# Thresholded attention on one core: a new table for the order of all instructions

## The chip, the core and the metric

The kernel runs on one core of one Trainium2 chip. Five engines work side by side: TensorE (PE, matmuls into PSUM), VectorE (DVE), ScalarE (ACT), GpSimd (POOL), and SyncE (SP), which here only issues transfers. The metric is the device time of one execution in microseconds.

## The reference

```python
batch, heads, seq, dim = 8, 12, 512, 64      # Q, K, V: float32, standard normal
scores = np.einsum('bhqd,bhkd->bhqk', Q, K) * scale            # scale = 1/8
weights = np.exp(scores - np.max(scores, axis=-1, keepdims=True))
weights = weights / (np.sum(weights, axis=-1, keepdims=True) + 1e-10)
weights = np.where(weights > threshold, weights, 0)            # threshold = 0.1
weights = weights / (np.sum(weights, axis=-1, keepdims=True) + 1e-10)
return np.einsum('bhqk,bhkd->bhqd', weights, V).astype(np.float32)
```

With 512 keys per query hardly any weight is over 0.1. A query row without such a weight has an output of zero.

## The kernel before

The kernel fills the output with zeros, finds the few query rows that can have a weight over the threshold, and computes those rows exactly. The 96 heads are 48 pairs, two pairs are a quad, and there are 24 quads. In what follows "quad q", "pair hp" and "key tile t" (0 to 3) number the work.

For each quad SP loads K (four transfers of 128 KB, `load_k`, line 330) and Q (`load_q`, line 334); for quads 0 and 1 the loads are split by pair, and some can stand on ACT's queue. PE transposes K in float32 (`do_ktr`, line 381), ACT or DVE evacuates it (`do_kev`, lines 389 and 391), POOL (for early quads also ACT or DVE) casts it to half precision (`do_kh`, lines 396, 398, 400). Q is cast first (`do_qcast`, lines 367, 369, 371), transposed in half precision (`do_qtr`, line 410) and evacuated by DVE (`do_qev`, line 416). Then come 192 score steps (`do_sc`, line 438: one key tile of one pair, two matmuls, one per head), 384 exponentials (`do_ex`: ACT at line 447 with the true exponential, DVE at line 449 with a bit trick that makes about the same number), and 192 row sum steps (`do_sm`, line 468: four matmuls that add the exponentials and their eighth powers, read from the same bits as bfloat16). A bound on the norms of Q and K needs squares of both ("bits", `do_bits`: POOL at line 425, ACT at 427, DVE at 429) and products with ones (`do_norms`, line 478).

The pairs form three groups of 24, 16 and 8. When a group's sums are complete, DVE (the first step, `do_y`, also on ACT: lines 486 and 488) compares the two sums (`do_d`, line 495; `do_fl`, line 500) and takes the eight best columns of each row (`do_mx`, line 504): the query rows that may survive. They are worked on in six stages of 8 pairs (three for group 0, two for group 1, one for group 2): an index product (`do_m`, line 513; `do_ix`, line 519), the index (`do_qi`, line 524), an indirect fetch of the query rows on POOL's queue (`do_gq`, line 534), their transposition with a mask (`do_xm`, line 541; `do_xev`, lines 547 and 549), the exact scores in float32 (`do_xqk`, line 556, 16 matmuls), the exponential with its sum (`do_xexp`, line 562), threshold and key number (lines 566 to 580), an indirect fetch of the value row (`do_gv`, line 585) and an indirect store to the output (`do_scatter`, line 600). The blank fills of the output ("z", `do_zero`, line 607, 512 KB each) stand on SP's queue.

Two helpers keep TensorE's clock up: eight warming steps of four matmuls on a blank tile (`do_warm`, line 340) at the start, and four spare products at the end (`do_spare`, line 344).

What sets the order: every one of the 1,326 steps is registered with its engines, its dependencies and the buffers that it takes and gives, and then issued one after the other as the string ORDER (line 13) says. Each word of it is a step's number in base 36 and a letter for the engine (P PE, V DVE, A ACT, G POOL, S SP, Q ACT's transfer queue, N none). So the table sets three things at once: the order on each engine's queue, which engine takes a step that several can do, and which buffer of a pool a step gets, since buffers are handed out first in, first out. Pools are short: seven PSUM banks ("one") for scores, transposes and stages, 32 buffers ("big") for K, Q and their forms. Transfers use eight semaphores in turn, so that the ninth waits for the landing of the first.

Of the kernel before, what the change touches and what calls it, by code (L numbers as in the profile page):

```python
# [9 lines left out]

ORDER = """6N fS gQ 1G hS 18Q 7P 24S 22S 8P 3G 5V 23S 16Q 9P 17S aP jP 2tS bP kA lV 2uS iG mA 2vS nP cP oV 3qS pV qP 3pS 12P sA rV yP dP 10A zV 26P 13A 25G 27V 1aP 28A 1bA 29V 0G 2aP uP 1cV 19A eP 2bV wA 52S 2cV 1eP 14V 2wG vA 2hP 1fV 1dG tP 2jA 11P 1gV 31P 2iA 1xG 2xP 32V 1tP 2yV 2zA 2lP 33V 30A 1pP 1vV xP 1qA 1uV 38P 2mA 3rG 3aV 1hP 1rA 53S 3sG 1wP 39V 1jA 3gP 1yG 6fS 15P 1iA 2nV 34P 3iA 3hV 2dP 36A 3cP 2fV 2eA 3tP 3kG 3dV 35A 6gS 2oP 3uA 3vV 1lP 2pP 7sS 1zN 1mA 1nV 3yP 3eA 3wG 3zV 56P 2qA 40V 3xG 57A 58V 45P 41P 46A 47V 1oP 54G 49P 42A 2rV 1kP 55G 4bA 2gP 43V 4lP 4aA 59G 95S 5bP 4nA 37P 3lG 5cV 1sP 4mA 4dP 5dV 4tP 4eA 4fV 6jP 4vA 4uV 5qP 6kA 3bP 5aG 3mN 5sV 2kP 6lA 5mP 6hG 5uP 5rA 5nV 5eP 6iG 7tS 5oA 4gP 5wV 4cP 5fA 6mG 5iP 96S 5gV 6oP 5vA 6nG aiS 4oP 6pV 5kA 4pP 6qV 7wP 5jA 7nV 6vP 7xA 7yV 5lP 7oG 5xP 4rA 44P 6xV 5yP 6wA d8S 5tP 60V 5zA 7fP 6zP 4qA 7hV 5hP 3jP 7gA 70V 7jP 99P 7kA 71V 77P 9aA 5pP 7uG 78V 7iP 79A 6yP 7vG 7lV 66P 9bA 7zG 81P 67A 7bP 82V 68A 3fP 97G 6rP 83V 7dA 98G ajS 2sP 7cV 6sA 88P 80G 8cP bwS 6tV 89A 7mP 9cG 9eP bvS 8eV 8aA 73P 9dG 8dA 7eP 7pN 9fV amP 4xG 75A 9gV 74V a5P anA 8kP a7V aoA 4wP 69P 8mA d9S 7aP 8lV 62P apG a6A 84P fzS 64V 8gP 86A 76P elS 85V 72P 8hA 48P 4hP 8iA 63V 9lP 4jA a8P akG 9mV 87P 9nA 9pP alG 4iV 8sP 9rA 8fP 6aG 8tV 8oP 9qA arP 8pA 65P asV a9P 8uA atV 8nP aaV 8qA auP 4yG 9hP awA abV b6P emS avA 4kP 9jV 61P 4sP 9iA fyS b7V b2P b8A dcP bxG 4zN b3V b4A acP byG ddA a1P deV bzP a2A aqG a3V 9xP 9oP daG c0V c1A ayP 9yA 8bP b0V 9zA a4P c2G biP 9tP azV 6bG bkA c4P 9sP c5V bjA axP 9vV 8vP hbS 9uA 8wP baP c6V 8xA 8jP 8yV dfG 6cN cfP bcA epP bbV dgG cgA cbP chV eqA dbG beP cdA 8rP ccV c3G 9kP bgA dhP bfV adG cjP erA 9wP hcS diV ckA cvP clV czP 21S cxA 8zP djV ciP d0A ioS ceP d1V esG ecP cwA bmP g0G edV dkP eeA bhP etG bdP boA bnV b9P dmA enG crP dlV doP ctA cmP k1S eoG csV e4P dqA cnP dpV e5A b1P 6uP efP coA e6V euP cpA dsP bqV e8P evV dtA cyP g1G e9V drP duA blP g2P ewV eaA brV exP g3A g4V fdP bsN aeG bpP ffA cuP ezV ipS f5P feA flP lfS f7V f6A cqP dnP k2S ebP eyV fmA g5G afN g7P fnA f1P g8V f9P hdG f2A dvP g9V e7P heG faA f3V c7P giP g6G fbA c9V foP a0P gjA 90G f0P gkV c8A fhP hfP fiV fjA isP hgV hhA b5P itA leS 91G iuV dwP gaP dxA gqP gcV fcP gbA f8P f4P grV dyA d2P h2P gsV iqG 92N geP h3A fpP ekS h4V ivG dzP ggA fgP gdP 51S irG frV gfA gtP gmP fqV hiG hkP goA guP k3G hlV ghP gwA fsP hmV glP hjG gnA e0P gvV gyP 2G e2A hnP gzV gpP e1A gxP h0V caP hpA ixP hzP hoA iyV lgG i7P i1A h1P izV h5P k4G e3P i8A i9V fkP lhG i0A qvS hvP xtV j4P iwG hwA 20P tlS 7qP xuV j5A 4G btP 3nP msS hxA k5P xvN xwV piS j6A j8P xxV 50P k6A mrS agP 93P k7A xyV jcP j9A xzP 6dP y0V jeA ydV i3P xrV y2G jdA hqP i2P y1V i5A jaV ibP 3oS ifP i4A jfP k8G igV o5S joP idA hyP ijG icV ihA yeP hrP jqA yfV iiP ygV htA hsV kaP liP jpA kbV jgP yhG ikV ljA iaP kcV ilN jkP lkA jhV khP jiA huP egG jmV y3P kiA kjA jlV jsP j0P h6A y4V klP j1V kkP y5P k9G ehA j2V ysV kmA jtV eiN juA jwV ktP knA o4S mtG yiP kuV y6A d3G kpP yjV h7A l1P kvV ykP y7V l2V krA h8N l3A y8V phS llG kqA lnP lmG ylA kxP loV mvP muG kzA ymV lpV ieP d4G kyA ynV ksP jnP mwA uxS m2P mxV meP m4A m6P m3V l4P mgA koP pjG n0P d5N mfV m7A lyP m8A myG jrP n1V o8P m0V lzA o6G s8S kdP n2V o9A o7G maP quS kfV j7P oaA mzG jvP mcV keA n7P jxG n3P mbA n8V m1P m5P n4A l0P n5V ytP n9A nbP plP s7S yuV ncV ndA lqP obG jyN pmA lsV nnP mmG pnA mdP n6P yvV lrV noA nvP l5P npA nxV odP 7rS l6A neP oeV m9P ocG l7A 6eS nwV luP miP pkG lwA d7S ofV nqP j3P mjV mkA qwG ogP mqS pqP lvA ohV poG nrP 94S oiA mhP qxG prV naP nsA tkS osP psV ywG ooP ntA otV jbP ltP opA kgP oqV ptP ouA mnG qyP yoV puV pvA q1P qzA l8P q2V orP q3A lxP r0V ldS p0P owP ppG p1A okP moN y9V p2V pwP oyA s9G mlP i6P omV uyS olA saG p8P qdP oxV paA sbP nzG qfA p9V nfP buS scA ozP ngV onP qeA ojP sdV qlP nhA q5P r1G k0S yxP qmV q6A r2G q7V r3P yyA p4P seG qnA r4V nuP haS p5A ftG q9P r5V pxP qbA qaV jjP p3P pzA q8P pyV riP p6A njP rkV sgP rjA yqG nyP shV nkA qgP ryP siV nlA r6P srP tmG rzA yzP ssV r8A ybG stV r7A s0V p7P yaV z0A ovP fuV waS reP ypV fvN tfV rqP rgA toP z1V rfV sfG rrA pbP z2V uzG r9P rsA qoP tnG rmP tpV tqA t3P s6S roA q4P t5V ttP trG t4A o3S nmP tuV tsG rnA qhP ahS ruP tvV qjA v0G niP rwV pgS u4P qiA ycG twP z3V u5V rvA kwP q0P rpP txA u6V t7P o0G tyA raP t9V uoP t8A rlP uqV qcP rbA v1P rcA upV u8P v2A usG rtP o1N z4V v3V sjP tjS u9A szP skV wbS uaA rdP rxP t0A t1V fxS snP u0P slA v4G s1P spV inS rhP u2A qkP utG u1V uwS v6P z7A svP v7V weP swA z8V wfA ugP v8V z9N smP wgA sxV v5G u3P suP soA z5G uhV ucP vtP uiA tzP ueV t6P udA w1P zaV vuA vxP sqP vzA ufP w2V wcG ujP vyA taP vvV whG v9P w9S qtS w3A vpP wiG vbV vaA vdP u7P wdG vrV vfA vwP ubP s2G vqA zbV wjP ukP veA vsP wkV uuN umA vlP ulV vhP vmA vgP wlV w0P vjA vnV s3G tbP wuP viA tdV unP voP wwA t2P wvV tcA wmP xmS x2P zcV woA x6P yrG s4N vcP x4A x8V w4P urP x3A wxP wnV wyP x7A wqP x0V zdP wzA x5P syP zeV wrA vkP pcV xeP wsA zgG xaP xgV teP xfA wpP x9P xcV xbA x1P xhP pdA zrV wtP z6G w5V xdP zsP 106A peN zhP ztV 107V d6P ziA ejP zvG zjP 108N 109V 10aV 10bV zuV 10cP zkA 10dV zwP zlV 10fG zmV jzP zxA s5P l9A zyP znV zfV zoV xiA zpG laA 10gP pfP 10hV zzA lbN 10iP qpA 100V 101V zqG 103V tgV 102V imP thN fwP 10jA xnP 104G o2P w6A uvP 10kV 10lV lcP tiP h9P qqA w7N w8P 10mV 10eV 10sV xjV 10oG 10nV xkN qrN 10rV xlP mpP qsP xoP xsV xpP xqP 105G 10qV 10tV 10pG"""


class Plan:
# [11 lines left out]
    def order(self):  # L28
        words = ORDER.split()
        if words:  # L30
            at = {"P": "PE", "V": "DVE", "A": "ACT", "G": "POOL", "S": "SP", "Q": "ACTQ", "N": "NONE"}
            seq = [(int(w[:-1], 36), at[w[-1]]) for w in words]
        else:
            seq = self.simple()
        assert sorted(i for i, _ in seq) == list(range(len(self.ops))), "the table is of other steps"
        idle = {p: list(range(k)) for p, k in self.pools.items()}
        self.held, done = {}, set()
        for i, e in seq:
            name, engs, _, deps, _, fn, takes, gives, _ = self.ops[i]
            assert e in engs and all(self.ids[d] in done for d in deps), name  # L40
            for pool, key in takes:
                self.held[pool, key] = idle[pool].pop(0)
            fn(e)
            for pool, key in gives:
                idle[pool].append(self.held[pool, key])
            done.add(i)
# [807 lines left out]
```

## Time and profile before

| | us |
|---|---|
| median of 3 runs | 172.88 (172.75 to 175.5) |
| the profiled execution | 172.14 |
| its span, first to last instruction | 170.4 |
| PE busy | 159.7 (94%) |
| ACT busy | 151.5 (89%) |
| DVE busy | 150.3 (88%) |
| POOL busy | 132.2 (78%) |
| DMA: moved | 38.27 MB, mean 225 GB/s |

Times in the rows are in microseconds from the span's start, except "mean ns". A busy PE is not a PE at its peak, since matmuls overlap in the records. Instructions of ACT and DVE overlap a little too, so that a row that merges many ("x18") shows what one costs when they follow each other closely. In square brackets stand the idle time of the engine before the row and what ended it.

### The profile page before, as it was taken

The numbers are of one execution on the slowest core, as the hardware profiler recorded it, in microseconds if no ns is written. First come the engines' busy times: TensorE is split into PE (matmuls) and PEld (weight loads), VectorE is DVE, ScalarE is ACT, GpSimd is POOL, SyncE is SP. The second block draws the span as 40 slices with busy tenths as digits, with TensorE's granted clock in tenths as the row PEclk, the third lists the DMA queues.
The fourth block names the chain that finished last, engine by engine and source line by source line (L and its number), as shares of the span: only waits on it lengthen the run. The fifth ranks groups of instructions, "written<-read, shape, count | busy, mean of one in ns | idle before, by whom it ended". The sixth has DMA issues, their size and how long they took to land.

```text
span 170.4 us, 5820 instructions
## 1 busy us (share of the span) xinstructions
PE 159.7 (94%) x2190; PEld 62.4 (37%) x2190; DVE 150.3 (88%) x349; ACT 151.5 (89%) x298; POOL 132.2 (78%) x200
## 2 busy tenths in 40 slices
PE   4999999999999999999979999999999999989970
PEld 1342544442444244333332344433343423332330
DVE  5489999989999999998989899999899999976570
ACT  3499999999999999899999999999899999956830
POOL 8549995795989759967693999999789969554362
PEclk9999999999999999999999999999999999999998
DMA  5999998969999797996995789999999997000000
GB/s 133 271 287 183 260 252 227 243 145 313 256 260 215 187 255 165 311 322 220 313 281 170 162 212 232 310 390 258 371 306 388 328 417 309 5 3 5 6 4 9
DMA packets 67453, 38.27 MB, mean 225 GB/s; under 512 B 51941, under 2 KB 64349, under 8 KB 67424
## 3 DMA queue, kind: packets, MB, share of 16 engines
q1 hardware_dynamic: 65520, 37.23, 78.4%
q10 hardware_dynamic: 1328, 0.52, 1.2%
q8 instruction: 17, 0.28, 0.7%
q0 software_dynamic: 576, 0.13, 0.5%
q14 instruction: 12, 0.10, 0.2%
HBM read 25.56 MB, written 12.78 MB: 225 GB/s over the span
## 4 chain that ended last, share of the span: by engine, by line
PE 69%; SPq 13%; DMA 7%; issue 3%; DVE 3%; ACT 2%; POOL 1%; ACTq 0%; POOLq 0%; DVEq 0%
PE sum L468 25%; PE one L438 25%; SPq L330 11%; PE one L556 5%; PE one L381 5%; DMA big<-in_K_dram 4%; PE one L410 3%; DMA big<-in_Q_dram 3%; SPq L334 2%; PE one L541 2%; PE one L478 2%; PE one L519 1%; POOL out_dram L600 1%; ACT e L447 1%; DVE junk L570 0%
## 5 line engine op out<-in xcount | busy, mean ns | idle before, releaser
L447 ACT ACTIVATE e<-one 128x512 f16<-128x512 f32 x232 | 119.6, 648 | 2.3 <-PE one L438 2.0
L449 DVE TENSOR_SCALAR e<-one 128x512 uint16<-128x512 f32 x152 | 97.0, 683 | 3.1 <-PE one L438 2.0
L438 PE MATMUL one<-big 64*128 64x512 f16 x384 | 67.2, 384 | 0.9 <-issue 0.3
L468 PE MATMUL sum<-e,w_s 128*32 128x512 f16 (+1 forms) x768 | 58.2, 384 | 0.0
L425 POOL TENSOR_TENSOR big<-big 128x512 bf16<-128x512 f16 x54 | 54.8, 1041 | 2.9 <-DVE big L429 2.8
L371 POOL CAST qh<-big 128x512 f16<-128x512 f32 x47 | 28.1, 616 | 14.4 <-PE one L438 5.1
L438 PEld LDWEIGHTS <-big 64*128 64x128 f16 x384 | 17.4, 95 | 34.3 <-issue 28.1
L400 POOL CAST big<-big 128x512 f16<-128x512 f32 x45 | 27.1, 615 | 2.7 <-DVE cut L566 1.3
L468 PEld LDWEIGHTS <-w_s 128*32 128x32 f16 (+1 forms) x768 | 15.5, 95 | 33.1 <-issue 27.9
L416 DVE COPY big<-one 128x512 f16<-128x512 f16 (+1 forms) x52 | 19.4, 398 | 2.1 <-PE one L410 1.6
L389 ACT COPY big<-one 128x512 f32<-128x512 f32 (+1 forms) x35 | 19.7, 600 | 1.3 <-PE one L381 1.2
L381 PE MATMUL one<-identity_f,big 64*128 64x64 f32 x384 | 18.3, 229 | 1.0 <-DMA big<-in_K_dram 0.7
L381 PEld LDWEIGHTS one<-identity_f,big 64*128 64x128 f32 x384 | 15.8, 140 | 6.7 <-POOL mask_x L225 1.6
L534 POOL DMA_INDIRECT qs<-in_Q_dram,idx x6 | 6.4, 1065 | 8.2 <-DVE idx L524 2.8
L391 DVE COPY big<-one 128x512 f32<-128x512 f32 (+1 forms) x17 | 10.5, 624 | 2.4 <-PE one L381 1.7
L556 PE MATMUL one<-big,xq 128*32 128x512 f32 x96 | 11.5, 597 | 0.6 <-issue 0.4
L410 PEld LDWEIGHTS <-qh 64*128 64x128 f16 x384 | 8.5, 95 | 8.2 <-issue 5.4
L410 PE MATMUL one<-identity_h,qh 64*128 64x64 f16 x384 | 10.7, 192 | 0.3 <-DVE big L391 0.2
L427 ACT ACTIVATE big<-big 128x1024 bf16<-128x1024 f16 x10 | 10.2, 1059 | 0.0
L600 POOL DMA_INDIRECT out_dram<-vr,idx x6 | 6.2, 1034 | 3.8 <-DVE cut L566 2.1
L585 POOL DMA_INDIRECT vr<-in_V_dram,idx x6 | 6.3, 1056 | 2.3 <-DVE oks L758 0.9
L562 ACT ACTIVATE one<-one 128x512 f32<-128x512 f32 x6 | 3.5, 582 | 4.2 <-PE one L556 4.2
(85 smaller groups left out, 81.3 us busy)
## 6 DMA issues: line engine op xcount, KB each, us to landing
out_dram<-zero SPq DMA_DIRECT2D x24, 512.0 KB
big<-in_K_dram SPq DMA_DIRECT2D x94, 128.0 KB
big<-in_Q_dram SPq DMA_DIRECT2D x22, 512.0 KB
big<-in_Q_dram SPq DMA_DIRECT2D x3, 256.0 KB
big<-in_K_dram ACTq DMA_DIRECT2D x2, 128.0 KB
big<-in_Q_dram ACTq DMA_DIRECT2D x1, 256.0 KB
qs<-in_Q_dram,idx POOLq DMA_INDIRECT x6, 3.8
vr<-in_V_dram,idx POOLq DMA_INDIRECT x6, 3.8
```

Source lines behind the costliest of these rows:

```text
L371: behind(nc.gpsimd.tensor_copy(dst, src))
L381: nc.tensor.matmul(dst[i][:, c:c + D], lhsT=src[ps, n0 + n, r, :], rhs=identity_f32[ps, ps], is_transpose=True, start=True, stop=True)
L389: nc.scalar.copy(dst, src)
L400: behind(nc.gpsimd.tensor_copy(dst, src))
L410: nc.tensor.matmul(dst[i][:, c:c + D], lhsT=src[ps, n0 + n, r, :], rhs=identity_h[ps, ps], is_transpose=True, start=True, stop=True)
L416: nc.vector.tensor_copy(qk_b[big("qk", q)][:, 0, n0:n0 + k, i * SO * D:(i + 1) * SO * D], src)
L425: behind(nc.gpsimd.tensor_tensor(out=dst[:, n, :], in0=src[:, n, :], in1=src[:, n, :], op=ALU.mult))
L438: nc.tensor.matmul(one[at("one", ("sc", hp, t, h))][:], lhsT=qk[ps, 1, n, t * P:(t + 1) * P], rhs=qk[ps, 0, n, :], start=True, stop=True)
L447: nc.scalar.activation(dst, src, ACTF.Exp, scale=scale, bias=-11.0 * math.log(2.0))
L449: nc.vector.tensor_scalar(dst.bitcast(u16), src, scale * LOG2E * 1024.0, 4096.0, op0=ALU.mult, op1=ALU.add)
L468: nc.tensor.matmul(dst[32 * j:32 * j + 32, :], lhsT=w, rhs=x, start=first, stop=False, skip_group_check=True)
L556: nc.tensor.matmul(one[at("one", ("xs", x))][sl, :], lhsT=xq_b[at("xq", x)][:, n, sl], rhs=kt_b[big("kt", quads[j])][:, n, :], start=(n == ...
```

## The change

The only line that changes is the table itself; the functions, the tiles and the steps stay as they are.

```diff
--- before.py
+++ after.py
@@ -10,7 +10,7 @@
-ORDER = """6N fS gQ 1G hS 18Q 7P 24S 22S 8P 3G 5V 23S 16Q 9P 17S aP jP 2tS bP kA lV 2uS iG mA 2vS ...
+ORDER = """6N fQ hS 1G gQ 24S 7P 18Q 22S 8P 9P 0G 5V 23S aP 16S 17Q bP cP 2vS dP iA 2tS jP nP kA lV ...
```

Counted from both tables, these steps are on another engine or in another stretch. "Start" is ahead of the first exponential in the table, "middle" from it to the last one, "tail" behind it.

| steps | before | now |
|---|---|---|
| exponentials ACT / DVE | 232 / 152 | 231 / 153 |
| squares ("bits") ACT / DVE / POOL | 10 / 11 / 27 | 8 / 14 / 26 |
| of these in the tail, ACT / DVE | 7 / 3 | 6 / 5 |
| evacuations of half a K tile in the middle, ACT / DVE | 3 / 3 | 5 / 1 |
| casts of K or Q by ACT: start / middle | 1 / 2 | 3 / 0 |
| casts of K or Q by DVE in the middle | 1 (K) | 1 (Q) |
| casts of K or Q by POOL | 92 | 92 |
| y of group 2 | ACT | DVE |
| transposed queries evacuated (xev) ACT / DVE | 3 / 3 | 4 / 2 |
| transfers on ACT's queue | 3 | 4 |
| warming steps ahead of the first transposes | 4 of 8 | 7 of 8 |
| score steps ahead of the second tile's transposes | 3 | 4 |
| exponentials left on ACT / DVE when stage 2's exact scores are issued | 2 / 3 | 3 / 2 |
| exponentials between the three fills ahead of the last K load and that load | 16 to 23 | 3 to 7 |

The first place is ACT's queue at the start of the program. `big` are loaded tiles, `qh` the cast Q, `one` PSUM banks, `e` the exponentials. Before:

```order
L330 DMA big_114<-in_K_dram 128x4x64
L334 DMA big_115<-in_Q_dram 128x2x256
L330 DMA big_114<-in_K_dram 128x4x64
L389 ACT_TABLE_LOAD
L389 COPY big_118<-one_107 128x256
L396 CAST big_119<-big_118 128x512
L447 ACTIVATE e_148<-one_112 128x512
```

Of the change, the same place:

```order
L330 DMA big_114<-in_K_dram 128x4x64 x2
L334 DMA big_115<-in_Q_dram 128x2x256
L330 DMA big_114<-in_K_dram 128x4x64
L367 ACT_TABLE_LOAD
L367 CAST qh_146<-big_115 128x512
L389 COPY big_118<-one_107 128x256
L396 CAST big_119<-big_118 128x512
L367 CAST qh_147<-big_116 128x512
L447 ACTIVATE e_149<-one_107 128x512
```

Both halves of K's first tile now come over ACT's queue, one after the other (the first Q tile has SP's first place instead), and two casts of Q stand ahead of the first exponential.

The second place is DVE's queue behind its last exponential: `y` holds the row sums of the last group, `idx_178` stage 4's index, `idx_179` stage 5's. Before:

```order
L449 TENSOR_SCALAR e_153<-one_110 128x512
L513 TENSOR_TENSOR m_166<-vals_164,mask_m 64x128
L429 TENSOR_SCALAR big_119<-big_141 128x512
L524 TENSOR_SCALAR idx_178<-one_106,base 128x1
L495 SCALAR_TENSOR_TENSOR y_162<-y_162,sum_113 64x512
L500 SCALAR_TENSOR_TENSOR y_162,count<-y_162,far_row 64x512
```

Of the change, the same place:

```order
L449 TENSOR_SCALAR e_156<-one_112 128x512
L429 TENSOR_SCALAR big_135<-big_116 128x512
L488 TENSOR_SCALAR y_162<-sum_113 64x512
L524 TENSOR_SCALAR idx_178<-one_110,base 128x1
L495 SCALAR_TENSOR_TENSOR y_162<-y_162,sum_113 64x512
L500 SCALAR_TENSOR_TENSOR y_162,count<-y_162,far_row 64x512
```

The step y (line 488) has come over from ACT and stands ahead of stage 4's index; the small product `m_166` was issued earlier.

The third place is POOL's queue in the same stretch: fetches of queries (`qs`), of values (`vr`) and the store of stage 2 (`vr_196`). One piece of the difference, before with -, now with +:

```order
 L534 DMA qs_183<-in_Q_dram,idx_177 128x64
+L534 DMA qs_184<-in_Q_dram,idx_178 128x64
 L600 DMA out_dram<-vr_196,idx_176 49152x64
-L534 DMA qs_184<-in_Q_dram,idx_178 128x64
 L534 DMA qs_185<-in_Q_dram,idx_179 128x64
 L585 DMA vr_197<-in_V_dram,idx_177 128x64
```

Stage 2's store stands behind stage 4's query fetch now, where it stood ahead of it.

## Rows read from the trace of the kernel before

**Rows 1.** Windows A:B: length, then PE, PEld, DVE, ACT, POOL busy, PEclk, DMA share, GB/s
```profile
7.20:10.00 2.80, 2.63 (x34) 1.02 (x30) 2.18 (x5) 2.53 (x6) 0.94 (x2) 1.00 1.28 241
7.20:149.70 142.50, 140.29 (x2006) 55.27 (x2004) 135.57 (x265) 139.28 (x280) 118.27 (x176) 1.00 0.92 258
149.70:170.40 20.70, 14.70 (x150) 5.25 (x141) 11.29 (x39) 9.95 (x16) 9.08 (x9) 0.97 0.03 6
```
**Rows 2.** Groups by line and form: busy us, mean ns of one, idle before
```profile
L391 DVE COPY big<-one 128x256 f32<-128x256 f32 x4 | 1.7, 423 | 1.8 <-PE one L381 1.7
L389 ACT COPY big<-one 128x256 f32<-128x256 f32 x4 | 1.5, 374 | 0.8 <-PE one L381 0.8
L396 ACT CAST big<-big 128x512 f16<-128x512 f32 x2 | 1.2, 620 | 0.4 <-DVE big L391 0.4
L367 ACT CAST qh<-big 128x512 f16<-128x512 f32 x1 | 0.6, 621 | 0.0
L429 DVE TENSOR_SCALAR big<-big 128x512 int32<-128x512 int32 x11 | 5.2, 472 | 0.1
```
**Rows 3.** Timeline (start us, us, instruction): the same instruction several times in a row
```profile
69.51 3.67 DVE L449 TENSOR_SCALAR e<-one 128x512 uint16<-128x512 f32 x6
140.56 9.06 ACT L447 ACTIVATE e<-one 128x512 f16<-128x512 f32 x18
155.60 2.95 ACT L427 ACTIVATE big<-big 128x1024 bf16<-128x1024 f16 x3
```
**Rows 4.** Timeline of the start, all engines
```profile
1.61 1.90 PE L340 MATMUL one<-blank,w_n 128*32 128x512 bf16 x16 [1.61 <-DVE w_n L210]
...
2.29 0.55 ACTq L330 DMA_DIRECT2D big<-in_K_dram  x1
...
2.87 1.28 ACT L389 ACT_TABLE_LOAD   x1 [2.87 <-issue]
...
4.21 0.69 PE L381 MATMUL one<-identity_f,big 64*128 64x64 f32 x8 [0.71 <-DMA big<-in_K_dram]
...
6.56 1.46 PE L438 MATMUL one<-big 64*128 64x512 f16 x6
...
7.18 0.69 DVE L449 TENSOR_SCALAR e<-one 128x512 uint16<-128x512 f32 x1 [0.67 <-PE one L438]
...
7.96 0.62 PE L340 MATMUL one<-blank,w_n 128*32 128x512 bf16 x4
...
10.13 0.40 PE L340 MATMUL one<-blank,w_n 128*32 128x512 bf16 x4
```
**Rows 5.** Timeline at stage 2's exact scores, PE and ACT
```profile
121.10 1.92 PE L556 MATMUL one<-big,xq 128*32 128x512 f32 x16
123.12 0.58 ACT L562 ACTIVATE one<-one 128x512 f32<-128x512 f32 x1 [0.66 <-PE one L556]
```
**Rows 6.** Timeline of the tail: POOL, ACT, DVE and PE
```profile
149.53 1.06 POOL L600 DMA_INDIRECT out_dram<-vr,idx  x1 [0.31 <-issue]
...
151.08 0.68 ACT L486 ACTIVATE y<-sum,small 64x512 f32<-64x512 f32 x1 [0.53 <-PE one L519]
151.20 0.22 DVE L524 TENSOR_SCALAR idx<-one,base 128x1 int32<-128x1 f32 x1 [0.73 <-PE one L519]
...
151.69 1.02 POOL L534 DMA_INDIRECT qs<-in_Q_dram,idx  x1 [1.10 <-DVE idx L524]
...
154.64 0.65 PE L541 MATMUL one<-mask_x,qs 128*64 128x256 f32 x4
...
155.24 1.00 POOL L534 DMA_INDIRECT qs<-in_Q_dram,idx  x1 [2.53 <-DVE cut L566]
```
**Rows 7.** SP's queue; a landing in the chain of waits; K's transposes by line
```profile
117.13 3.79 SPq L607 DMA_DIRECT2D out_dram<-zero  x3
122.18 3.18 SPq L330 DMA_DIRECT2D big<-in_K_dram  x4
...
29.57 7.55 DMA big<-in_K_dram
...
L381 PE MATMUL one<-identity_f,big x384: 216/222/367, 4.2 to 135.0; 64*128 64x64 f32 x192
```

2 lines of the change are left out of this document (1 added, 1 removed).

## The prediction

> **What bounds the kernel now.** I read the windows of the trace first, in three stretches: up to the first exponential at 7.2 us, to the end of the last one at 149.7, and the rest. In the middle 142.5 us ScalarE (ACT) is busy for 139.28 us and VectorE (DVE) for 135.57 [rows 1]. PE shows 140.29, but its matmuls overlap in the records, so that this says little of its load. The exponentials (line 447 on ACT, 449 on DVE) can run on either engine, so the two are one pool of work, and the middle lasts about half of their joint work plus their waits. Recorded idle time there is 3.2 us on ACT and 6.9 on DVE, 5.1 us on average: the most that a better order could win in the middle while it moves no work out. The DMA engines are 92% busy in the same stretch [rows 1], so transfers have little slack as a whole; but the view of waits names none for which ACT or DVE waited there.
>
> Then the timeline of the tail, 149.7 to 170.4. Nothing there is a matter of throughput: both engines are busy for about half of it [rows 1]. It is one chain: the last row sums, y, d, the search for survivors, the index product, the query fetch, the exact scores of stages 4 and 5, the value fetch, the store. So the order can change three things: how soon the first exponential starts, how much work and waiting lies in the middle, and how long the chain behind the last one is.
>
> **The change, part by part.** The sum is made against the profiled execution, 172.14 us, of which 170.4 are the span. That execution is 0.74 us faster than the median of the runs shown, 172.88.
>
> *The head.* Three rows set when the first transposes may start. Before, they begin at 4.21 us, on the arrival of K; the 16 warming products took 1.90 us from 1.61 [rows 4]. Now 28 of them stand ahead of the transposes: 28 × 1.90/16 = 3.33 us, so until 4.94. Also the second half of K's first tile has become the second transfer on ACT's queue, where it was the first before; this delays it towards the same time. And ACT issues four transfers instead of three, 0.55 us more [rows 4], ahead of the table load of 1.28 us, which now ends at 2.87 + 0.55 + 1.28 = 4.70; the cast of Q behind it takes 0.62 [rows 2] and ends at 5.32, before the transposes do. So transposes and first exponential come 4.94 − 4.21 = 0.73 us later, at about 7.9. Against this: in the 2.8 us from 7.2 to 10.0 ACT idles for 0.27 us and DVE for 0.62 [rows 1], since only three score products stand ahead of the next transposes; now there are four, which feed each engine with four exponentials. I count the average of that idle time, 0.45, as won. Head: +0.73 − 0.45 = **+0.28 us** (bounds: 0.73 if nothing is won back, −0.45 if the later start is made up by work that was done meanwhile).
>
> *Work in the middle.* By the table of step counts, between the first and the last exponential ACT loses one exponential ((9.06 − 0.65)/17 = 0.49 back to back [rows 3]), one squaring pass (0.95, half of 2.95 − 1.06 [rows 3]) and two casts (0.62 each [rows 2]; two casts of Q now stand ahead of the first exponential, in time in which ACT only waited), and takes over two evacuations of half a tile (0.37 each [rows 2]): −0.49 − 0.95 − 1.24 + 0.74 = −1.94 us. DVE gains one exponential ((3.67 − 0.68)/5 = 0.60 [rows 3]) and one bit pass (0.47 [rows 2]), loses two evacuations (0.42 each [rows 2]), and swaps one cast for another: +0.23 us. Together −1.71, half of it on each engine: **−0.86 us**. It is covered by nothing else: the work goes to time before the first exponential, and to the tail, where both engines have room. GpSimd (POOL) does one squaring less and as many casts; it is busy for 118.27 of 142.5 us, so its share doesn't decide.
>
> *Waits in the middle.* The clearest one is at stage 2's exact scores: PE spends 1.92 us on 16 fp32 products (line 556) and ACT waits 0.66 us for them [rows 5]. In the old order ACT has two exponentials left when that product is issued, in the new one three. One more is 0.49 us of the 0.66; DVE has one fewer, so I count half, **−0.24 us**. The other waits I can't read from the order; each is some tenths of a microsecond. Bounds for them: the average idle time of 5.1 us can shrink or grow by half, ±2.5; I take 0, since the order's other features (score products issued ahead, evacuations split in two) stay alike.
>
> *The tail.* Stage 2's store moves behind stage 4's query fetch on POOL's queue. Before, the store starts at 149.53 and takes 1.06 us, so it is over at 150.59; the fetch starts at 151.69, and what it waits for is DVE's index, written from 151.20 on [rows 6]. So the store wasn't in the way, and taking it away wins **nothing**. Behind the fetch it lies between 152.8 and 153.9, in the gap that POOL has until the next fetch at 155.24 [rows 6], and nothing of the chain waits for it. If that gap were gone, it would cost its 1.06 us.
>
> What does touch the chain is y, the first step on the sums of the last group. It moves from ACT to DVE, and DVE computes stage 4's index right behind it and ahead of d. Before, y ran on ACT from 151.08 and the index on DVE from 151.20, side by side [rows 6]. Now the index waits for y's 0.68 us: it starts at about 151.76, 0.56 later, and d is pushed by the distance from y's end, about 0.14 (the index takes 0.22 and overlaps its neighbours). The fetch is 0.56 later too; stage 4's mask product started at 154.64 [rows 6], held by the index product of stage 5 ahead of it on PE, which is only 0.14 later. Bounds: +0.14 if the fetch still has room, +0.56 if it has none; I take **+0.25 us**, nearer the first since PE was held by the other one. The squares left for the tail (11 where there were 10) run beside the chain on both engines.
>
> Sum: +0.28 − 0.86 − 0.24 + 0 + 0.25 = −0.57, 172.14 − 0.57 = **171.6 us**.
>
> **A rule weighed.** In the head, four warming products take 0.62 us at 7.96 and 0.40 at 10.13 [rows 4]: by its durations the first is TensorE at 1.2 GHz and the second at 2.4, though the column of the granted clock shows 1.00 in that stretch [rows 1]. PE had been busy with gaps before: until 3.51, then from 4.21. The Trainium skill ("TensorE: Matmul & The Clock Gate", Part 1) says that the low clock is the default and that sustained activity releases it. This trace agrees that it starts low. The new order puts the warming products in one unbroken run of 3.33 us; by the rule the clock may rise before the first score products, by the row it rises where it did. That is the second rival.
>
> **The rivals.**
> 1. *The order takes out more waits than can be read from it.* For it: 5.1 us of idle time on average, in many small pieces, which is what an order can remove. Against: the work is the same, and the longest pieces have other causes. Half of it gone: 171.6 − 2.5 = 169.1 us.
> 2. *The clock rises early.* The eight transposes take 0.69 us from 4.21; at the higher clock a group of four warming products goes from 0.62 to 0.40, by a third [rows 4]. A third of 0.69 and of the 0.62 us from the score's issue at 6.56 to the exponential at 7.18 is 0.44: 171.2 us.
> 3. *A transfer comes late* (the other side). Three blank fills of the output stand ahead of the last K load on SP's queue in both tables, but the new one issues them 13 to 16 exponentials later, close to that load. Three such took 3.79 us of SP's queue; before, the load followed them from 122.18 to 125.36 and was transposed by 135.0 [rows 7]. If all of their time is added, the issue ends at 129.15, 5.85 us ahead of the end of its use. This decides if a landing takes over about 5.5 us; a K load in the busy phase took 7.55 [rows 7]. Then the last scores are 2.0 us late: 173.6. Against: before, the issue ended 9.6 us ahead of the last transposes, and SP's queue need not be late by all of the 3.79.
> 4. *The clock falls or rises late.* No warming products are left between the first scores and the next transposes. Three more microseconds at 1.2 GHz would cost at most half of them: 173.1. Against: PE is dense there.
> 5. *The change does nothing*: the moved store is hidden before and after, and the rest cancels: 172.1.
>
> **How the numbers follow.** Forecast 0.45; rival 1 0.20; rival 2 0.12; rival 3 0.10; rival 4 0.05; rival 5 0.08. Differences under 2% can't be told from none on this kernel, whose own runs lie 1.6% apart. 2% below the median of before is 169.4, which about two thirds of rival 1 (0.13) and a little of the forecast and of rival 2 (0.03) pass: faster 0.16. 2% above is 176.3, for which rival 3 would have to hit several loads, 0.06 with what is left of rival 4; same 0.78. The forecast's own terms span 170.4 to 172.8. The range takes in rival 1 at its centre and rival 3 to one microsecond beyond: 168.8 to 174.5.
>
> **What would show it right or wrong.** The first exponential at 7.5 to 7.9 us (a time near 7.2 speaks for rival 2). From there to the last one 141 to 142 us, with ACT busy for about 2 us less in that stretch and no wait over 0.3 us before stage 2's exponential of exact scores. From the last exponential to the end 20.7 to 21.3 us, with d starting about 0.1 us after where y leaves it and POOL's store of stage 2 in a gap. Wrong: a wait of PE for a transfer of K beyond 20 us (rival 3), or idle time of ACT and DVE in the middle that differs by more than 2 us from 3.2 and 6.9 (rival 1, or its opposite).

## The result and the profile after the change

The changed kernel takes 172.25 us (median of 20 runs, 170.92 to 173.16), the kernel before 173.56 us (20 runs, 172.75 to 175.5, the three shown ahead of the prediction among them). The ratio is 0.992, with a 95% interval of 0.990 to 0.994: 0.8% or 1.3 us faster, no difference by the bound of 2%. The forecast was 171.6 us and no change. On a second chip the experiments give the same kernel 1.007 times the time of the one before (1.003 to 1.010). So the sum came out, several of its terms did not, and on the second chip the sign of the result is the other one.

The profiled execution after takes 172.26 us, with a span of 170.5. The windows of its trace, from the first exponential to the last and from there to the end, with busy time and instructions of each engine, granted clock, DMA share and GB/s, answer to [rows 1]:

```profile
core 0: us, PE busy (x) PEld busy (x) DVE busy (x) ACT busy (x) POOL busy (x), PEclk, DMA share, GB/s
8.98:150.15 141.17, 139.82 (x1998) 55.38 (x1996) 136.01 (x267) 137.54 (x278) 116.80 (x177) 1.00 0.90 256
150.15:170.50 20.35, 14.34 (x150) 5.26 (x142) 11.45 (x41) 8.36 (x15) 9.27 (x9) 0.92 0.03 6
```

The first exponential starts at 8.98 us where it was at 7.18 [rows 4]. The middle is 141.17 us long where it was 142.5 [rows 1]; ACT does 1.74 us less in it and DVE 0.44 more. Their idle time there is 3.63 and 5.16 us, where it was 3.2 and 6.9. So the middle, ACT's work and the idle time lie where the prediction put them; the first exponential (forecast 7.5 to 7.9) comes too late, and the tail, 20.35 us where it was 20.7, is shorter than the 20.7 to 21.3 of the forecast.

The start in the timeline of after (start, length, engine and line, operation; in brackets idle time and what ended it), with one row of the chain of work between:

```profile
0.75 1.33 ACTq L330 DMA_DIRECT2D big<-in_K_dram  x2
1.60 3.18 PE L340 MATMUL one<-blank,w_n 128*32 128x512 bf16 x28 [1.60 <-DVE w_n L210]
1.43 4.85 DMA big<-in_K_dram
6.42 0.69 PE L381 MATMUL one<-identity_f,big 64*128 64x64 f32 x8 [1.64 <-DMA big<-in_K_dram]
8.98 1.29 DVE L449 TENSOR_SCALAR e<-one 128x512 uint16<-128x512 f32 x2 [1.01 <-PE one L438]
```

The 28 warming products end at 4.78 us, as forecast (4.94). But the transposes then wait 1.64 us for the second half of K's first tile, the second transfer of ACT's queue, which lands at 6.28 (the first lands at 4.13). In the kernel before both halves were the first transfers of two queues, and the transposes began at 4.21 [rows 4].

The tail in the timeline of after answers to [rows 6]:

```profile
150.75 0.68 DVE L488 TENSOR_SCALAR y<-sum 64x512 f32<-64x512 f32 x1 [0.27 <-PE sum L468]
151.47 0.22 DVE L524 TENSOR_SCALAR idx<-one,base 128x1 int32<-128x1 f32 x1
151.72 0.69 DVE L495 SCALAR_TENSOR_TENSOR y<-y,sum 64x512 f32<-64x512 int32 x1
151.96 1.00 POOL L534 DMA_INDIRECT qs<-in_Q_dram,idx  x1 [2.31 <-DVE idx L524]
153.26 1.01 POOL L600 DMA_INDIRECT out_dram<-vr,idx  x1 [0.30 <-issue]
154.55 0.65 PE L541 MATMUL one<-mask_x,qs 128*64 128x256 f32 x4
```

The index stands between y and d (0.97 us from one to the other), and the store lies in POOL's gap, both as forecast. Not forecast: y starts 0.60 us after the last exponential's end; in the trace of before this was 1.39 us.

### The profile page after: what moved, and what is told of

The parts are those of the page before. It is cut to its first block, busy times and chain, and to the rows that moved or that the text cites. A ratio compares the mean times of both kernels' runs of the same rounds, so it can differ in the third digit from the quotient of the medians.

```text
span 170.5 us, 5813 instructions
## 1 busy us (share of the span) xinstructions
PE 159.4 (94%) x2190; PEld 62.8 (37%) x2190; DVE 150.8 (88%) x351; ACT 149.3 (88%) x297; POOL 130.1 (76%) x198
## 4 chain that ended last, share of the span: by engine, by line
PE 74%; DVE 12%; DMA 7%; ACT 3%; issue 1%; POOL 1%; ACTq 0%; DVEq 0%
PE sum L468 27%; PE one L438 26%; PE one L381 8%; DVE e L449 5%; DMA qs<-in_Q_dram,idx 4%; PE one L410 4%; PE one L556 3%; PE one L478 3%; DMA big<-in_K_dram 3%; ACT e L447 2%; PE one L541 1%; DVE nmax L491 1%; PE one L344 1%; DVE m L513 1%; DVE idx L524 1%
## 5 line engine op out<-in xcount | busy, mean ns | idle before, releaser
L468 PE MATMUL sum<-e,w_s 128*32 128x512 f16 (+1 forms) x768 | 59.4, 387 | 0.6 <-ACT e L447 0.4
L425 POOL TENSOR_TENSOR big<-big 128x512 bf16<-128x512 f16 x52 | 52.8, 1036 | 1.8 <-DVE big L429 1.3
L400 POOL CAST big<-big 128x512 f16<-128x512 f32 x47 | 28.1, 611 | 16.0 <-ACT big L389 4.4
L371 POOL CAST qh<-big 128x512 f16<-128x512 f32 x45 | 26.6, 611 | 6.3 <-DMA big<-in_Q_dram 3.3
L389 ACT COPY big<-one 128x512 f32<-128x512 f32 (+1 forms) x37 | 20.6, 598 | 2.9 <-PE one L381 2.7
L416 DVE COPY big<-one 128x512 f16<-128x512 f16 (+1 forms) x52 | 19.4, 398 | 1.7 <-issue 0.4
L391 DVE COPY big<-one 128x512 f32<-128x512 f32 (+1 forms) x15 | 9.7, 649 | 3.8 <-PE one L381 3.6
L410 PEld LDWEIGHTS <-qh 64*128 64x128 f16 x384 | 9.0, 97 | 7.6 <-issue 2.9
L410 PE MATMUL one<-identity_h,qh 64*128 64x64 f16 x384 | 11.3, 195 | 0.0
L427 ACT ACTIVATE big<-big 128x1024 bf16<-128x1024 f16 x8 | 8.2, 1057 | 0.0
L429 DVE TENSOR_SCALAR big<-big 128x512 int32<-128x512 int32 x14 | 6.5, 479 | 0.0
```

Source lines behind the costliest of these rows:

```text
L371: behind(nc.gpsimd.tensor_copy(dst, src))
L389: nc.scalar.copy(dst, src)
L400: behind(nc.gpsimd.tensor_copy(dst, src))
L410: nc.tensor.matmul(dst[i][:, c:c + D], lhsT=src[ps, n0 + n, r, :], rhs=identity_h[ps, ps], is_transpose=True, start=True, stop=True)
L416: nc.vector.tensor_copy(qk_b[big("qk", q)][:, 0, n0:n0 + k, i * SO * D:(i + 1) * SO * D], src)
L425: behind(nc.gpsimd.tensor_tensor(out=dst[:, n, :], in0=src[:, n, :], in1=src[:, n, :], op=ALU.mult))
```

## The experiments

Theory 1: the start is a loss, the middle the gain, the tail about nothing. Its rivals: the late K tile is absorbed, or the gain is in the start or in the tail. Where a table is joined from two, each step stands once, in the order of the second table for what is left. In the order's words P is PE, V VectorE, A ScalarE, G GpSimd, S and Q the DMA queues of SP and ACT.

### The first K tile: e1_k_first

f and g are the halves of the first K tile, h and 18 tiles of Q:

```diff
-6N fQ hS 1G gQ 24S 7P 18Q 22S 8P 9P
+6N fS gQ 1G hS 18Q 24S 7P 22S 8P 9P
```

> The changed kernel with one thing undone: the first six steps of the loads stand as in the kernel before, so the two halves of the first K tile are the first transfer of SP's and of ACT's queue, and the first Q tiles come second. Everything else, the 28 warming products too, stays. Theory 1 (the late second half of the first K tile costs at the start what the trace of after shows there, first transposes at 6.42 us and first exponential at 8.98): transposes start at about 4.9, when the warming products end, first exponential at about 7.5, and the time falls by 1.2 to 1.5 us against the changed kernel, ratio to the kernel before about 0.984. Rival (the start is absorbed: the later loads or the low clock until 17 us hold the pipeline anyway): first exponential earlier, but the ratio stays at about 0.992.

Measured: 170.97 us, 0.987 (0.983 to 0.991), between the two expectations. The timeline of its start:

```profile
1.60 3.18 PE L340 MATMUL one<-blank,w_n 128*32 128x512 bf16 x28 [1.60 <-DVE w_n L210]
4.71 0.62 PE L381 MATMUL one<-identity_f,big 64*128 64x64 f32 x8
7.30 2.48 DVE L449 TENSOR_SCALAR e<-one 128x512 uint16<-128x512 f32 x4 [0.53 <-PE one L438]
```

Transposes and first exponential stand where theory 1 put them, 1.7 us earlier. All of it goes through: the 16th exponential moves from 16.95 to 15.27 us, the 100th from 45.69 to 44.01, the last from 149.47 to 147.54. The later loads absorb nothing. By the ratios, 0.987 against 0.992, it is 0.9 us, but these two come from different sets of runs; a closer pair follows with e2.

### Start, rest and tail apart: e2_head_before, e3_head_after, e4_tail_after

```diff
-order: the changed table
+e2: before's table up to its 16th exponential, then the changed table
+e3: the changed table up to its 16th exponential, then before's table
+e4: before's first 1213 steps (the same set in both tables), then the changed table
```

> The order of the kernel before up to its 16th exponential, and behind it the remaining steps in the order of the changed kernel. Theory 1 (the start is a loss of the change, the middle its gain): the gain of the middle without the loss of the start, ratio to the kernel before about 0.984, the clock up at about 8.6 us as in the trace of before. Rival A (the start costs nothing): 0.992. Rival B (the change's gain comes from the start): 1.000. Where the joint itself costs a wait (it was made by no search) up to 0.5 us more.

> The counterpart: the changed order up to its 16th exponential, and behind it the remaining steps in the order of the kernel before. Theory 1: the loss of the start alone, ratio to the kernel before about 1.008 (1.4 us slower). Rival A (the start costs nothing): 1.000. Rival B (the gain comes from the start): 0.992.

> The order of the kernel before for its first 1213 steps, which are the same set of steps in both tables (all but the last 14 or so exponentials), then the tail of the changed kernel: y on VectorE instead of ScalarE, index and fetch of stage 4 ahead of d, store of stage 2 behind the fetch of stage 4. Theory 1 with the prediction's tail (+0.25 us): ratio 1.001. By the two traces (last exponential to end 20.7 before, 20.35 after): 0.998. Rival (the gain of the change lies in the tail): 0.992 to 0.994.

Measured: e2 0.985 (0.981 to 0.990), e3 1.009 (1.006 to 1.012), e4 0.998 (0.995 to 1.002). Theory 1 holds in all three, on the chip of e1: the changed start costs 0.65% (e2 against 0.992, from another set of runs) to 0.89% (e3 against 1, in one set), 1.1 to 1.5 us. e1 and e2, in one set too, take 170.97 and 170.89 us: putting back the loads alone is worth as much as putting back the whole start. The tail gives 0.3 us, which its interval can't tell from nothing. What is left, some 2.2 to 2.6 us, is the middle.

The windows of after and of e3, which have the same start, from the 16th exponential to the end of the last one (columns as above):

```profile
16.95:150.15 133.20, 132.08 (x1926) 52.02 (x1926) 128.81 (x251) 131.73 (x266) 112.68 (x169) 1.00 0.88 256
```

```profile
16.70:151.98 135.28, 133.56 (x1926) 52.71 (x1924) 129.47 (x250) 132.55 (x267) 111.06 (x168) 1.00 0.89 254
```

The changed order is 2.08 us shorter. ACT is busy 0.82 us less and DVE 0.66, on average 0.74. ACT's idle time falls from 2.73 to 1.47 us and DVE's from 5.81 to 4.39, on average by 1.34. The views of ACT's waits in these two windows, e3 first, name the largest piece of ACT's part: the exponentials of the exact scores of three stages, which wait for PE (us in total, times, longest).

```profile
ACT one L562 <- PE one L556: 1.8, 3, 1.0
```

```profile
ACT one L562 <- PE one L556: 0.3, 1, 0.3
```

In the trace of before it was 1.4 us. What takes out the rest was not broken down.

### The clock at the start: e5_k_first_16

e1 with fewer warming products ahead of the transposes (7 to 9 and a to e are the eight blocks of four):

```diff
 7P 8P 9P aP
-bP cP dP (transposes of K, then of Q)
+(transposes of K) bP (transposes of Q) cP dP
```

> The changed order with the first loads as before and, beyond that, with 16 warming products ahead of the first transposes as before: one block of four goes behind the first transposes of K, two behind those of Q. Theory 2 (a part of the start's loss is the granted clock, which in the trace of after and with the first loads put back was low until 17.06 and 15.36 us, in that of before until 8.55): the blocks that stand in the gaps bring the clock up for good before 12 us; from the first to the 16th exponential 7.2 to 7.7 us in place of 7.97; first exponential near 7.3 as before, since the cast of Q holds it; ratio to the kernel before 0.983 to 0.985. Rival (the low clock costs nothing there, ACT and DVE hold the pace): 7.97 and a ratio of 0.987. Second rival (the number of warming products ahead of the transposes matters itself): first exponential at 6.8.

This and the next three ran on another chip. Measured: 173.99 us, 1.007 (1.004 to 1.010); what that ratio means is settled only by e9. Its start, in the timeline:

```profile
6.49 1.47 PE L340 MATMUL one<-blank,w_n 128*32 128x512 bf16 x12
7.89 1.87 PE L438 MATMUL one<-big 64*128 64x512 f16 x8
8.54 1.92 DVE L449 TENSOR_SCALAR e<-one 128x512 uint16<-128x512 f32 x3 [1.45 <-PE one L438]
```

The clock rose for good at 9.54 us, and from the first to the 16th exponential it took 6.93 us in place of 7.97, as theory 2 has it. But with the block that already stood behind, twelve warming products are in a row ahead of the first scores. The score products start 1.0 us later behind them (7.89 against 6.88 in e1) and take longer to the first exponential, since e1's clock was up from 5.12 to 8.54: it comes 1.24 us later (8.54 against 7.30), and the 16th comes no earlier (15.47 against 15.27). The edit loses ahead of the first exponential what the clock gives back behind it.

### Single edits of the tail: e6_y_act, e7_store_ahead, and the kernel before: e8_before_again

```diff
-e6: y of the last group on VectorE
+e6: y of the last group on ScalarE
-e7: ... gq(stage 4) scatter(stage 2) ...
+e7: ... scatter(stage 2) ... gq(stage 4) ...
```

> The changed kernel with one step on another engine: y, the first step on the last row sums, runs on ScalarE as in the kernel before, at the same place of the order. By the prediction's tail term y on VectorE costs 0.25 us (bounds 0.14 to 0.56): stage 4's index then starts beside y and its fetch 0.4 us earlier, d follows y at once, and from y's start to the last store it takes 15.35 us as in the trace of before in place of 15.59. Expected: ratio to the kernel before about 0.990, 0.25 to 0.4 us less from the last exponential's end to the end than the 20.35 to 20.58 of the changed tail. Rival (the chain is held elsewhere, by the exact scores of stage 3 on PE): no change, 0.992. Other rival: y waits behind the squaring pass on ScalarE and comes later, 0.993.

> The changed kernel with the one edit of its title undone: the store of stage 2 stands ahead of stage 4's query fetch on GpSimd's queue, all else as in the changed kernel. By the prediction (the store is hidden before and behind the fetch) nothing changes: ratio to the kernel before 0.992, the store at about 149.7 us and the fetch at about 152.0 as in after. Rival (the store holds the fetch): the fetch comes up to 1.06 us later, ratio 0.995 to 0.998.

> The kernel before, unchanged, for a second profiled execution, since its first one (172.14 us) is faster than its median by 1.4 us. If that is the granted clock at the start: the clock comes up later than 8.55 us, and the first exponentials after that are later by some tenths. If it is the tail: from the last exponential's end to the end over 21 us in place of 20.7, with y starting 0.9 us behind the last exponential (held by the squaring pass ahead of it on ScalarE) or 1.4 as in the first. If it is the middle: the first to the last exponential over 143 us in place of 142.5.

Measured: e6 1.012 (1.007 to 1.016), e7 1.017 (1.012 to 1.021). Both are 2.2 to 2.5% above what was expected, and hardly through their edits: in e5, e6 and e7 alike it takes 20.2 to 20.3 us from the start of the 300th exponential to that of the 350th, in after, e1 and e2 19.5. (The expectation of e9 counts by merged rows and has 19.9 and 19.2.) e8, a single run at 173.6 us: clock up at 14.92 us, first to last exponential 143.3 us, tail 20.8, y 1.47 us behind the last exponential. The first profile of before had been lucky with the clock; the late y came again.

### The chip or the edit: e9 to e12

The changed kernel itself, e7, e6 and e2 once more, together. They ran on the chip of e5 to e8.

> The changed kernel, unchanged, beside the next two on the same chip. Three single edits of it were measured together on another chip than the first four kernels, and all three came out slower than the kernel before (ratios 1.007, 1.012, 1.017), with the same stretch lengthened: from the 300th to the 350th exponential 19.9 us in place of 19.1 to 19.2. Theory C (the chip does it, not the edits: on that chip reports of PE come late at some places, which the changed order bears worse): the changed kernel itself stands wherever its edits stand, 1.007 to 1.017 if this is such a chip, 0.992 if not. Theory E (the edits cost what was measured): 0.992 here, whatever the chip, and the edits behind it by 1.5 to 2.5%.

> The store of stage 2 ahead of stage 4's query fetch, all else as in the changed kernel, once more. Theory C and the prediction: equal to the changed kernel on the same chip within 0.3%, that is 0.5 us. Theory E: 2.5% slower than it, over 4 us. Between them: up to 0.8 us slower, if the report of the last row sums comes late behind the store, so that y starts 1.4 us after the last exponential's end in place of 0.6.

> y on ScalarE, all else as in the changed kernel, once more. Theory C with the prediction's tail term: 0.25 to 0.4 us, 0.2%, less than the changed kernel on the same chip. Theory E: 2% slower than it.

> The order of the kernel before up to its 16th exponential, then the changed order, once more: on the first chip it was the fastest, ratio 0.985. It should stand below the changed kernel by 0.6 to 0.9% on any chip, since the late first K tile costs the same 1.1 to 1.5 us; against the kernel before 0.985 where the changed one stands at 0.992, and 1.000 to 1.010 where that stands at 1.007 to 1.017.

| kernel | first chip | second chip |
|---|---|---|
| changed (under first chip: the result above) | 0.992 (0.990 to 0.994) | e9: 1.007 (1.003 to 1.010) |
| store of stage 2 ahead | not run | e10: 1.008 (1.005 to 1.011) |
| y on ScalarE | not run | e11: 1.007 (1.004 to 1.011) |
| before's start, changed rest | e2: 0.985 (0.981 to 0.990) | e12: 0.998 (0.994 to 1.002) |

That the result was taken on a chip like the first is read from its trace (last section). Theory C holds: the chip, not the edits. Theory E falls: e10 and e11 equal e9. The kernel of e7 and e10 is one, yet gave 175.92 and 174.94 us, 1.017 and 1.008, in two sets of runs on one chip, so differences under 1% between sets are not evidence by themselves. Each chip stands for one or two sets, so the ratios alone can't tell the chip from the moment; that all eight profiles of the second chip differ in one place from the five of the other kind (last section) is what speaks for the chip. e12 against e9, 0.9% in one set, is again the cost of the changed start.

Where the second chip takes its time, in the windows of e9 from the 16th exponential on:

```profile
15.65:150.37 134.72, 133.36 (x1926) 51.89 (x1926) 128.67 (x252) 131.86 (x265) 113.69 (x169) 1.00 0.90 257
150.37:172.00 21.63, 14.36 (x150) 5.25 (x142) 11.45 (x40) 8.36 (x15) 9.29 (x9) 0.96 0.03 5
```

The work is that of after, but ACT idles for 2.86 us in place of 1.47, and the tail is 1.28 us longer. Two places account for most of it: the 300th to the 350th exponential takes 1.08 us more, and in the tail one maximum comes 1.1 us late. In the timelines, first after and then e9, the copy of Q's transposes (L416) ahead of stage 2's exact scores and the maximum of the norms (L491) in the tail, with POOL's rows around them:

```profile
119.58 0.69 DVE L449 TENSOR_SCALAR e<-one 128x512 uint16<-128x512 f32 x1 [0.15 <-PE one L438]
120.28 0.82 DVE L416 COPY big<-one 128x512 f16<-128x512 f16 x2
...
164.53 1.01 POOL L600 DMA_INDIRECT out_dram<-vr,idx  x1 [0.38 <-DVE oks L758]
164.92 0.69 DVE L491 TENSOR_REDUCE nmax<-one 128x1 f32<-128x512 f32 x1 [0.64 <-PE one L478]
```

```profile
118.71 0.69 DVE L449 TENSOR_SCALAR e<-one 128x512 uint16<-128x512 f32 x1 [0.15 <-PE one L438]
118.76 1.06 POOL L585 DMA_INDIRECT vr<-in_V_dram,idx  x1 [0.16 <-issue]
120.49 0.82 DVE L416 COPY big<-one 128x512 f16<-128x512 f16 x2 [1.09 <-ACT e L447]
...
164.87 1.01 POOL L600 DMA_INDIRECT out_dram<-vr,idx  x1 [0.31 <-DVE oks L758]
166.43 0.69 DVE L491 TENSOR_REDUCE nmax<-one 128x1 f32<-128x512 f32 x1 [1.73 <-PE one L478]
```

In after the copy starts as DVE comes free, 0.47 us behind the start of PE's last transpose (119.81). In e9 that transpose starts at 118.94, DVE is free at 119.40, and the copy starts only at 120.49, 1.55 us behind it. The maximum starts 1.1 us later against PE's last norm product (1.53 us behind its start in place of 0.43). Both times POOL issues an indirect DMA just then. The maximum waits for PE alone, and the records of the reports (the semaphore updates by which an engine tells that it is done) show where the time goes: PE's last norm product ends at 164.87 in after and its report is recorded at 164.90; in e9 it ends at 165.28 and the report is recorded at 166.41, 0.02 us ahead of the maximum. The copy waits for PE, ACT and POOL, and the profile names ACT there; but it starts 0.16 us behind a report of PE both in after (120.12) and in e9 (120.33), though e9's last transpose had ended at 119.12. The same is seen at y, in the timelines of e9 and of e10, where the store is the row of POOL:

```profile
150.97 0.68 DVE L488 TENSOR_SCALAR y<-sum 64x512 f32<-64x512 f32 x1 [0.27 <-PE sum L468]
151.93 0.69 DVE L495 SCALAR_TENSOR_TENSOR y<-y,sum 64x512 f32<-64x512 int32 x1
```

```profile
150.54 1.02 POOL L600 DMA_INDIRECT out_dram<-vr,idx  x1 [0.30 <-issue]
152.04 0.68 DVE L488 TENSOR_SCALAR y<-sum 64x512 f32<-64x512 f32 x1 [0.98 <-PE one L519]
153.01 0.69 DVE L495 SCALAR_TENSOR_TENSOR y<-y,sum 64x512 f32<-64x512 int32 x1
```

With the store ahead, y starts 1.14 us behind the last sum's start, not 0.43: the moved store is worth 0.7 us at y on this chip. The tail of e10 is 22.24 us, that of e9 21.63; the medians of the two kernels, 174.94 and 174.55 us, can't be told apart.

## Why the prediction was right, and where it wasn't

1. *The head, +0.28, was mis-sized*: it is +1.1 to +1.5 us. The step that failed is the sentence that the second transfer on ACT's queue delays K's half "towards the same time" as the warming products' end. It was not worked out: that half lands at 6.28 us, 1.5 behind the products. The warming products' term was right for the transposes: with the loads put back (e1) they start at 4.71 (forecast 4.94). The first exponential stands at 7.30 there, earlier than the 7.5 to 7.9 of the forecast, with the clock up from 5.12 to 8.54. Of the 0.45 us won back some is plausible: with the clock up early (9.84 us, e9) the changed start needs 6.94 us from the first to the 16th exponential, before's 7.23 with the clock up at 8.55, 0.29 less; no run takes that feature alone.
2. *Work in the middle, −0.86, was about right*: ACT −1.74 and DVE +0.44 between the first and last exponentials (forecast −1.94 and +0.23), −0.65 on average; −0.74 between e3 and after.
3. *Waits in the middle, −0.24, were mis-sized*: −1.34 on the first chip, about half of rival 1. The mechanism named, more exponentials at hand when exact scores are issued, is seen: stage 2's wait falls from 0.66 to 0.25 us, under the 0.3 of the forecast. But it was counted for one stage of three and by half; over the three ACT's wait falls by 1.1 us against before. On the second chip most of the gain is gone: stage 2's wait is 0.84 us in e9, and seven profiles of the changed rest need 134.15 to 134.72 us from the 16th exponential to the last one's end (e12 134.67), the order before 134.65 in e8 and 135.28 in the first profile.
4. *The store, 0*: hidden on POOL's queue, as forecast; what its issue does to y's wait was overlooked. In the trace of before it starts at 149.53 and y at 151.08 [rows 6], 1.29 us behind the last sums' start. I read that gap as part of the chain; in the executions without an issue at that place it is 0.42 to 0.43.
5. *The tail, +0.25 for y, was right in its mechanism*: in e11 d follows y 0.26 us sooner than in e9 and stage 4's fetch is 0.42 us earlier against the last exponential. But the end came no sooner, since there the late maximum of the norms ends last (16.39 us behind the last exponential in e11, 16.07 in e9). On the whole (e4) the tail is 0.3 us shorter, which can't be told from nothing, where I had a loss.
6. *The rule weighed*: rival 2 did not come in after, where the clock rose at 17.06 us. In e1, e6 and e11, with the same unbroken run of 28 products, it rose at 4.5 to 5.1, was low again from 7.9 to 8.5 on, and rose for good at 14.7 to 15.4; in the other five executions with that run it did not rise before 9.84. The Trainium skill ("TensorE: Matmul & The Clock Gate", Part 1) says that the low clock is the default and that sustained activity releases it. The traces agree for three executions of eight, so on this kernel the run of 28 is no sure release. Of rival 4 there is up to 1 us in after, by the 7.97 us from the first to the 16th exponential against 6.94 in e9. Rival 3 was not seen: no wait of PE for K beyond 20 us.

So 171.6 was near 172.25 by luck, twice over. A loss of about 1 us that I missed in the start met a gain of about 1.1 that I missed in the waits. And the sum started from a profile of 172.14 us, 1.4 below the 173.56 of the kernel before: the change was forecast at −0.57 us and measured at −1.3, so that a base too low made up for a change too small. On the second chip the kernel takes 174.55 us, just beyond the upper end of the range, 174.5. The prediction's span of its own terms, 170.4 to 172.8, is not their sum: the bounds given for head and tail, with the other terms as they stand, make 170.7 to 172.3.

## What to carry to other kernels

Give the first operand's pieces the first place on different DMA queues: as the second transfer of one queue half a tile cost the whole kernel about 1 us here, and nothing later took it up. An order that is made to remove waits should be timed on more than one chip, since a gain of 0.8% on one was a loss of 0.7% on another. The best order found joins both: the start of the kernel before with the changed rest, 0.985 and 0.998, faster than the changed kernel on both chips (on the first by sets of runs that differ, on the second in one set) and not slower than the one before on either.

## What was not expected of the hardware

**Reports of PE that come late while GpSimd issues an indirect DMA, on one chip and not on another.** For three places the table gives the time from the start of PE's last matmul to the start of the DVE or ACT step that waits for it and, after the slash, when an indirect DMA's issue of about 1 us began against that matmul's start.

| execution | copy of Q's transposes | y | maximum of the norms |
|---|---|---|---|
| after | 0.47 / 0.14 | 0.43 / none | 0.43 / 0.04 |
| e1, first chip | 0.46 / 0.17 | 0.42 / none | 0.43 / −0.04 |
| e4, first chip | 0.40 / 0.35 | 0.43 / none | 0.43 / −0.03 |
| before, first profile | 0.40 / 0.41 | 1.29 / −0.26 | 0.56 / 0.68 |
| e8 (before), second chip | 0.40 / 0.41 | 1.36 / −0.26 | 0.57 / 0.68 |
| e9 (changed), second chip | 1.55 / −0.17 | 0.43 / none | 1.53 / −0.03 |
| e10, second chip | 1.26 / −0.16 | 1.14 / −0.37 | 1.54 / −0.03 |
| e12, second chip | 1.48 / −0.17 | 0.43 / none | 0.43 / 0.39 |

On the second chip each waiter is 0.6 to 1.5 us late when the issue began between 0.37 us before and 0.26 after, in all of its executions; from 0.39 on none is by more than 0.2. On the first chip the same overlap costs nothing, but for two cases in e3 that another step holds: y started at 0.79, when ScalarE's pass ahead of it ended, though the last sum's report is recorded 0.03 us behind that sum's end, inside the issue; and the copy started, with the issue at 0.37, at 0.74, behind an exponential of ScalarE. The records of the reports agree. At y and at the maximum, which wait for PE alone, the waiter starts 0.02 us behind the recorded report in every one of these executions but e3's y; where it is late, the report is recorded 0.7 to 1.5 us behind the end of PE's matmul, where it isn't, 0.02 to 0.16. And of the 31 to 39 reports of PE that are due inside the 18 issues of an execution, 33 to 40 are recorded inside them in after and e1 to e4, 15 to 23 in the first profile of before and e5 to e12; of ScalarE's 25 to 29 it is 26 to 29 and 13 to 18. So the two profiles that were compared first came from chips of different kinds. That the issue holds the reports is the reading that fits all of these; it was not tried by moving an issue alone at the copy or the norms, only at y (e10), and why the chips differ stays open. That VectorE itself is held during the issue doesn't fit: the report is late already, and y on ScalarE (before, e8) is late as well.

**The clock's rise is not the order's alone.** The times of its rise are those of the records of the granted clock, which begin with the first rise, so that the column PEclk shows 1.00 in windows ahead of it. Where they begin early the column tells both levels, 2.4 GHz as 1.00 and 1.2 as 0.50, as in two windows of e1 (columns as above):

```profile
5.12:8.54 3.42, 2.24 (x26) 0.68 (x23) 2.15 (x6) 3.12 (x6) 0.61 (x1) 1.00 1.25 264
8.54:15.36 6.82, 6.58 (x68) 3.12 (x68) 6.04 (x16) 4.88 (x13) 4.23 (x10) 0.50 1.25 257
```

With the same first 16 exponentials it rose for good anywhere from 9.84 us (e9) to 17.77 (e7), and in the kernel before at 8.55 and 14.92. From the first to the 16th exponential that is 6.94 to 7.97 us in the changed start and 7.23 to 8.69 in the one before, so 1 to 1.5 us of a single profile can be this.
